# Hybrid RG-LRU, gMLP and gated FFN block: the up products of the FFN chained in single PSUM banks, split weights kept in DRAM

## The chip, the cores and the metric

One core of one Trainium2 chip runs the whole program once. The metric is device microseconds of an execution (us), the median over runs.

## The reference, cut to what matters

Tokens 2048, width 1024, inner FFN width 3072, float32 throughout. The mixer (RG-LRU and gMLP) makes x, and the FFN follows:

```python
y = concat(RMSNorm(y_lru), RMSNorm(y_gmlp)) @ W_out
x = x + gate_m * RMSNorm_post(y)
h = rmsnorm(x, g_ffn_pre) * (1.0 + sc_f) + sh_f      # sc_f, sh_f, gt_f: parts 3 to 5 of c_act @ w_ada
up = causal_depthwise_conv(h @ w_up, ffn_conv_w, ffn_conv_b)   # width 3
g_ff, v_ff = split(up, 2)                            # 3072 gate and 3072 value columns
y = (gelu(g_ff) * v_ff) @ w_down
x = x + gt_f * rmsnorm(y, g_ffn_post)
```

## The kernel before, in words

**Products.** A float32 operand is split into a high and a low part of a reduced type: a cast on ACT (`split`, L129) and a subtraction on DVE (L134). Each product of two operands is then three matmuls, high by high, high by low and low by high (`mm3`, L170 to L172; in the FFN L926 to L928), each 128x128 by 128x512.

**Stages.** The mixer works on four chunks of 512 tokens; its last product is `mixer_out` (tiles `o`), and the last two chunks leave their result in DRAM (`o2d`), to be normalized and added to x later by `late_rms` and `late_post` (tiles `ol`, L575, L576; result in `x2d`). The FFN works on two chunks C of 1024 tokens, each as two halves of 512 tokens. For each C come first 24 *pairs* (`up_pair`; f counts them), a gate block and a value block of 128 columns, whose result goes to DRAM (`gd`), then `down(C, 0)` and `down(C, 1)`, each 24 x 8 products that accumulate in eight banks.

**One pair.** Two halves of the tokens, two halves of the contraction and two column blocks are a 2x2 by 2x2 block product, made with seven products instead of eight (the scheme of Strassen and Winograd). On the side of the tokens it takes h11, h12, h22 and the sums s1 to s4, which `h2_task` makes once for each C: a load of x2d, the normalization (L840, L841), sums on DVE, splits. On the side of the weights it takes three blocks and four sums t1 to t4, which `up_weights` makes for each pair: two loads of 512 KB (`wug`, `wuv`; L900, L901), four sums on POOL (L905, L906, L910, L913), seven splits. A product is 4 x 3 matmuls, a pair 84. Results lie in two PSUM tiles `upa` and `upc` of two banks each, out of a pool of four such tiles (all eight banks). Three ACT copies and five DVE additions (L934 to L948) put them together to `Rg` and `Rv`; `conv` (L886 on ACT, L888 twice on DVE, L890 for the chunk's last two tokens), a gelu (L951), a product (L952) and the store to `gd` (L953) end the pair.

**Order.** The program is written with generators in the background (`start`), which `tick` advances by a step at fixed points of the main loop, and a scheduler orders each engine's instructions; `high_priority` moves loads and splits ahead. SP issues nearly all DMAs, in order. The main sequence stands at L1041 to L1072: h2_task(0, 0) beside the mixer's product for chunk 2, h2_task(0, 1) after that for chunk 3, then the pairs of C = 0 with `late_rms(3)` and `ada_task(5)` (the last part of c_act @ w_ada, eight steps on DVE, L268 and L270) in the background; the `late_post`s beside down(0, 0); the normalizers of chunks 2 and 3 and then h2_task(1, ...) beside down(0, 1).

Of the kernel before, what the change touches and what calls it, by code (L numbers as in the profile page):

```python
# [15 lines left out]
P = 128  # L16
# [7 lines left out]
NF = 24  # L24
# [16 lines left out]
def block_kernel(ctx: ExitStack, tc: tile.TileContext, xt, cols, rows, wada, wada_r, win_k, win_s, win_v, wgate, wsp, wout, wup, wdown, out):  # L41
# [8 lines left out]
    ps = ctx.enter_context(tc.tile_pool(name="ps", bufs=4, space=bass.MemoryType.PSUM))  # L50
# [209 lines left out]
    def ada_task(m, pause=0):  # L260
# [566 lines left out]

    H2 = {}
    OPS = ("11", "s2", "12", "s1", "s3", "s4", "22")

    def h2_task(C, i):

        ops = H2.setdefault(C, {o: [None, None] for o in OPS})
        r = [rx[2 * C], rx[2 * C + 1]]

        def get(t, j, name):
            x = load_x(x2d, 2 * C + t, j, name, t4)
            for b in range(2):
                d = 2 * j + b
                vec.scalar_tensor_tensor(out=x[:, b], in0=x[:, b], scalar=sf[:, d:d + 1], in1=r[t], op0=ALU.mult, op1=ALU.mult)  # L840
                act.activation(out=x[:, b], in_=x[:, b], func=AF.Identity, bias=shf[:, d:d + 1])  # L841
            return x

        def put(o, x):
            hl = h4(f"h{o}_{C}{i}h"), h4(f"h{o}_{C}{i}l")
            split(hl[0], hl[1], x, "act")
            ops[o][i] = hl

        n = f"xf{C}{i}"
        a11 = get(0, i, n + "a")  # L850
        put("11", a11)
        yield
        a21 = get(1, i, n + "b")
        yield
        a22 = get(1, i + 2, n + "c")
        put("22", a22)
# [286 lines left out]
```

## Time and profile before

| what | value |
|---|---|
| median of 3 runs | 2361.22 us (2359.91 to 2363.95) |
| the profiled execution | 2354.39 us |
| its span | 2352.6 us |
| its mean granted TensorE clock | 0.957 of full speed |
| PE busy | 2102.8 us, 89% of the span |
| DVE, ACT, POOL busy | 70%, 42%, 23% |

The profile shows one execution. The span runs from its first to its last instruction. Busy PE time is the union of matmuls whose records overlap, so the pace is read from start to start.

### The profile page before, as it was taken

Reading aid. Unit: us, or ns where it says so; the run is one execution under the profiler, and the core shown is the slowest. Engines: PE = TensorE matmul, PEld = TensorE weight load, DVE = VectorE, ACT = ScalarE, POOL = GpSimd, SP = SyncE. Lnnn points to the kernel's source line nnn. Section 1 sums busy time; section 2 is a strip of 40 time slices with the busy share of each in tenths; the row PEclk is TensorE's granted clock in tenths of the full one; section 3 lists DMA queues with packets and bytes.
Section 4 is the critical chain, followed back from the end, with each engine's and each line's share of the span. In section 5 each row is a group of like instructions: output and inputs, shape, how many; then the busy total and the mean of one; then the engine's idle time right before and its main releaser. Section 6 shows DMA issues by size and latency. Waiting matters only on the chain.

```text
span 2352.6 us, 23905 instructions
## 1 busy us (share of the span) xinstructions
PE 2102.8 (89%) x9008; PEld 1698.9 (72%) x9008; DVE 1643.5 (70%) x1854; ACT 986.8 (42%) x1226; POOL 541.2 (23%) x344
## 2 busy tenths in 40 slices
PE   4898979999777898999989989979999999899995
PEld 3786868788555677777777768857777777778784
DVE  7688797986637777787766668587777777643634
ACT  3464645425433434444443345434444444432422
POOL 4443434343112222222200100032322223000000
PEclk8999989999787999999999989989999999999997
DMA  7677587675441222222226736431222212344542
GB/s 297 240 289 262 187 298 278 228 260 197 173 159 63 72 90 77 76 81 72 90 99 224 259 107 245 149 116 66 78 72 81 75 69 81 102 140 152 196 154 72
DMA packets 117428, 354.32 MB, mean 151 GB/s; under 512 B 10816, under 2 KB 10944, under 8 KB 117312
## 3 DMA queue, kind: packets, MB, share of 16 engines
q1 hardware_dynamic: 110400, 327.62, 40.0%
q0 software_dynamic: 6912, 25.17, 2.8%
q8 instruction: 71, 1.16, 0.2%
q14 instruction: 45, 0.37, 0.1%
HBM read 281.45 MB, written 71.30 MB: 150 GB/s over the span
## 4 chain that ended last, share of the span: by engine, by line
PE 62%; DVE 24%; ACT 6%; issue 4%; DMA 4%; POOL 0%; SPq 0%; DVEq 0%; ACTq 0%; POOLq 0%
PE dn L170 7%; PE dn L171 7%; PE dn L172 7%; DVE a L888 6%; PE upc L926 6%; PE upc L928 6%; PE upc L927 5%; PE upa L926 4%; PE upa L927 4%; PE upa L928 4%; ACT a L886 2%; DVE w L134 1%; DVE Rv L946 1%; DVE Rg L948 1%; DVE ada_m L270 1%
## 5 line engine op out<-in xcount | busy, mean ns | idle before, releaser
L170 PE MATMUL dn<-gh,wd_h 128*128 128x512 f32 x768 | 301.3, 393 | 10.9 <-ACT wd_h L129 6.0
L171 PE MATMUL dn<-gl,wd_h 128*128 128x512 f32 x768 | 300.2, 392 | 0.0
L172 PE MATMUL dn<-gh,wd_l 128*128 128x512 f32 x768 | 277.3, 392 | 11.1 <-DVE wd_l L134 11.1
L134 DVE TENSOR_TENSOR wd_l<-wd_r,wd_h 128x1024 fp32r<-128x1024 f32 x96 | 121.0, 1260 | 195.3 <-ACT wd_h L129 186.0
L905 POOL TENSOR_TENSOR wt<-wuv,wug 128x512 f32<-128x512 f32 x48 | 64.6, 1347 | 836.6 <-DMA wuv<-in_wup_dram 583.3
L129 ACT CAST wd_h<-wd_r 128x1024 fp32r<-128x1024 f32 x96 | 101.3, 1056 | 252.4 <-PE dn L171 238.9
L129 ACT CAST wt<-wt 128x512 fp32r<-128x512 f32 x144 | 89.5, 621 | 268.1 <-PE upc L928 241.9
L172 PEld LDWEIGHTS dn<-gh,wd_l 128*128 128x128 f32 x768 | 145.4, 189 | 44.4 <-DVE wd_l L134 14.0
L170 PEld LDWEIGHTS dn<-gh,wd_h 128*128 128x128 f32 x768 | 145.3, 189 | 44.2 <-ACT wd_h L129 7.7
L888 DVE SCALAR_TENSOR_TENSOR a<-Rv,prm,a 128x1023 f32<-128x1023 f32 x96 | 154.4, 1608 | 19.4 <-ACT a L886 18.6
L171 PEld LDWEIGHTS dn<-gl,wd_h 128*128 128x128 f32 x768 | 145.3, 189 | 30.2
L888 DVE SCALAR_TENSOR_TENSOR a<-Rg,prm,a 128x1023 f32<-128x1023 f32 x96 | 123.1, 1282 | 36.5 <-ACT a L886 35.7
L134 DVE TENSOR_TENSOR w<-wug,w 128x512 fp32r<-128x512 f32 x96 | 76.8, 800 | 72.7 <-ACT w L129 72.7
L134 DVE TENSOR_TENSOR wt<-wt,wt 128x512 fp32r<-128x512 f32 x144 | 117.6, 817 | 9.5 <-ACT wt L129 8.7
L129 ACT CAST w<-wug 128x512 fp32r<-128x512 f32 x96 | 59.8, 622 | 123.8 <-PE upa L928 110.6
L913 POOL TENSOR_TENSOR wt<-wug,wt 128x512 f32<-128x512 f32 x48 | 69.4, 1445 | 92.7 <-DVE wt L134 92.7
L886 ACT ACTIVATE a<-Rg,prm 128x1024 f32<-128x1024 f32 x48 | 59.7, 1243 | 58.8 <-DVE Rg L948 57.6
L906 POOL TENSOR_TENSOR wt<-wuv,wt 128x512 f32<-128x512 f32 x48 | 77.7, 1618 | 3.5
L952 DVE TENSOR_TENSOR a<-a,a 128x1024 f32<-128x1024 f32 x48 | 59.6, 1241 | 24.8 <-ACT a L951 24.8
L926 PE MATMUL upc<-hs_10h,wt 128*128 128x512 f32 x96 | 39.6, 414 | 40.6 <-DVE Rg L948 35.6
L886 ACT ACTIVATE a<-Rv,prm 128x1024 f32<-128x1024 f32 x48 | 59.8, 1246 | 31.9 <-DVE Rv L946 28.3
L134 DVE TENSOR_TENSOR gl<-gr,gh 128x1024 fp32r<-128x1024 f32 x48 | 60.0, 1250 | 17.9 <-PE upc L928 9.3
(602 smaller groups left out, 5855.8 us busy)
## 6 DMA issues: line engine op xcount, KB each, us to landing
wd_r<-in_wdown_dram SPq DMA_DIRECT2D x96, 512.0 KB, 4.3
wug<-in_wup_dram SPq DMA_DIRECT2D x48, 512.0 KB, 3.2
wuv<-in_wup_dram SPq DMA_DIRECT2D x48, 512.0 KB, 3.3
gd<-a SPq DMA_DIRECT2D x48, 512.0 KB, 2.6
gr<-gd SPq DMA_DIRECT2D x48, 512.0 KB, 3.5
wada<-in_wada_r_dram SPq DMA_DIRECT2D x32, 512.0 KB, 4.3
win_h<-kept_s SPq DMA_DIRECT2D x30, 512.0 KB, 5.9
win_l<-kept_s SPq DMA_DIRECT2D x30, 512.0 KB, 6.7
```

The costliest lines, as they stand in the source:

```text
L129: act.copy(out=hi, in_=src)
L134: (leng or vec).tensor_tensor(out=lo, in0=src, in1=hi.bitcast(F32), op=ALU.subtract)
L170: pe.matmul(out=out, lhsT=wh, rhs=mh, start=first, stop=False)
L171: pe.matmul(out=out, lhsT=wh, rhs=ml, start=False, stop=False)
L172: pe.matmul(out=out, lhsT=wl, rhs=mh, start=False, stop=last)
L886: act.activation(out=a, in_=R, func=AF.Identity, scale=w[2], bias=col("ffn_conv_b", blk))
L888: vec.scalar_tensor_tensor(out=a[:, s:], in0=R[:, :FT - s], scalar=w[t], in1=a[:, s:], op0=ALU.mult, op1=ALU.add)
L906: pool.tensor_tensor(out=t2, in0=b22, in1=t1, op=ALU.subtract)
L913: pool.tensor_tensor(out=t2, in0=b21, in1=t2, op=ALU.subtract)
L926: pe.matmul(out=bank, lhsT=wh, rhs=mh, start=not more and k == 0, stop=False, skip_group_check=more)
L927: pe.matmul(out=bank, lhsT=wh, rhs=ml, start=False, stop=False, skip_group_check=more)
L928: pe.matmul(out=bank, lhsT=wl, rhs=mh, start=False, stop=k == 3, skip_group_check=more)
```

## The change

Five things, here in the order of the program:

1. **The end of the mixer.** `h2_task` becomes `h2_plain` (normalizes x, splits h11, h12, h21, h22, and stores the four normalized tiles to a new DRAM tensor `hs`, with DMAs that ACT issues) and `h2_sums` (loads them back and makes s1 to s4, for C = 0). h2_plain(0, 1) and h2_sums(0, 0) run beside mixer_out of chunk 3.
2. **Plain first pairs.** f = 0 and 1 of C = 0 are made by `up_plain` with eight products (96 matmuls), which need no sums; h2_sums(0, 1) runs beside them.
3. **Chained pairs.** For the FFN the PSUM pool is closed and a new one of eight single banks opened. A pair takes three banks. In the first, product 11 is copied out (m1), s2 t2 is added and the sum copied out (x0), s3 t3 is added and read by DVE (Rv), 22 t4 is added and copied out (Rg): each is the sum of what came before in the bank. The second takes s1 t1 (copy m5) and s4 22, the third 12 21. That is four ACT copies and three DVE additions a pair. `up_phase` interleaves one pair's end with the next pair's start.
4. **Kept pieces.** In C = 0, from f = 2, each of a pair's seven split pieces is stored to DRAM (`wkd`, 512 KB each). In C = 1, from f = 2, `up_weights` loads the seven pieces, with no sum and no split.
5. **Late work.** `late_rms(3)`, both `late_post`s, the normalizers of chunks 2 and 3 and ada_task(5) start at f = 3 of C = 0. h2_sums(1, 0) and h2_sums(1, 1) run beside down(0, 0) and down(0, 1). down uses eight single banks and evicts each by itself; ada transposes go in two halves.

The diff, cut to its core:

```diff
+    def h2_plain(C, i):
+        for q, (o, t, j) in enumerate((("11", 0, i), ("12", 0, i + 2), ("21", 1, i), ("22", 1, i + 2))):
+            x = normed(C, t, j, f"xf{C}{i}{o}")
+            put(C, i, o, x)
+            act.dma_start(out=hs[C, i, q], in_=x)
+            yield
+    def h2_sums(C, i, get, plain=()):
+        a21 = get(1, i, "21")
+        a22 = get(1, i + 2, "22")
...
+        vec.tensor_tensor(out=a22, in0=a22, in1=a21, op=ALU.add)
+        put(C, i, "s1", a22)
...
+    def from_store(C, i):
+        def get(t, j, o):
+            x = lp.tile([P, 2, 512], F32, tag="ld", name=f"hs{C}{i}{o}")
+            sync.dma_start(out=x, in_=hs[C, i, ("11", "12", "21", "22").index(o)])
...
     def up_weights(C, f):
+        if C == 1 and f >= PLAIN:
+                for q, k in enumerate(PIECES):
...
+                    sync.dma_start(out=w[k].bitcast(F32), in_=wkd[f, q])
+            return w
...
+        if C == 0:
+            for q, k in enumerate(PIECES):
+                sync.dma_start(out=wkd[f, q], in_=w[k].bitcast(F32))
...
+    def up_pair(C, f):
+        w = up_weights(C, f)
+        pa = bank(f"upa{n}")
+        prod(C, pa, "11", w["11"])
+        act.copy(out=m1, in_=pa)
+        pc = bank(f"upc{n}")
+        prod(C, pc, "s1", w["t1"])
+        act.copy(out=m5, in_=pc)
+        yield
+        prod(C, pa, "s2", w["t2"], more=True)
+        act.copy(out=x0, in_=pa)
+        pb = bank(f"upb{n}")
+        prod(C, pb, "12", w["21"])
+        vec.tensor_tensor(out=Rg[:, :512], in0=pb, in1=m1, op=ALU.add)
+        prod(C, pc, "s4", w["22"], more=True)
+        vec.tensor_tensor(out=Rv[:, :512], in0=pc, in1=x0, op=ALU.add)
+        prod(C, pa, "s3", w["t3"], more=True)
+        vec.tensor_tensor(out=Rv[:, 512:], in0=pa, in1=m5, op=ALU.add)
+        v = conv(C, NF + f, Rv)
+        yield
+        prod(C, pa, "22", w["t4"], more=True)
+        act.copy(out=Rg[:, 512:], in_=pa)
...
-    drain(*lt)
-    drain(*start(h2_task(0, 1)))
-    start(late_rms(NC - 1, q), ada_task(5, 2))
+    nt = start(h2_plain(0, 1), h2_sums(0, 0, from_store(0, 0)))
+    O, q3 = mixer_out(NC - 1, True)
+    drain(*lt, *nt)
+    mixer_ps.close()
+    banks.append(ctx.enter_context(tc.tile_pool(name="pf", bufs=8, space=bass.MemoryType.PSUM)))
+    st = start(h2_sums(0, 1, from_store(0, 1)))
+    for f in range(PLAIN):
...
+        up_plain(0, f)
+    drain(*st)
+    up_phase(0, PLAIN, lambda f: start(late_chunks(), ada_task(5, 1)) if f == PLAIN + 1 else None)
```

**PE, between two pairs of C = 0.** The names give tile, chunk and pair: `upc0_15` is the second PSUM tile of pair 15, `hs1_00h` the high part of s1. Before, from pair 15 to pair 17, which share a PSUM tile (the first two products of pair 16 stand ahead of these rows):

```order
L926 MATMUL upc0_15_6947<-hs3_00h_4347,wt3_0_15_6936 128x512 [waits Activation_49]
...
L926 MATMUL upc0_15_6947<-hs4_00h_4431,w22_0_15_6939 128x512 [waits DVE_49]
...
L926 MATMUL upc0_15_6947<-h22_00h_4235,wt4_0_15_6943 128x512 [waits DVE_49]
...
L928 MATMUL upc0_15_6947<-h22_01h_4737,wt4_0_15_6943 128x512
L926 MATMUL upc0_17_7227<-hs1_00h_4270,wt1_0_17_7212 128x512 [waits DVE_49,Activation_49]
```

And now, around the start of pair 16:

```order
L971 MATMUL upa0_16_7340<-h11_00h_4153,w11_0_16_7308 128x512 [waits PE_49]
L972 MATMUL upa0_16_7340<-h11_00l_4154,w11_0_16_7308 128x512
L971 MATMUL upa0_15_7191<-hs3_00h_4674,wt3_0_15_7177 128x512 [waits Activation_49]
...
L973 MATMUL upa0_16_7340<-h11_00h_4153,w11_0_16_7308 128x512 [waits DVE_49]
...
L971 MATMUL upc0_16_7355<-hs1_00h_4543,wt1_0_16_7312 128x512
...
L971 MATMUL upa0_15_7191<-h22_00h_4290,wt4_0_15_7181 128x512 [waits DVE_49]
...
L971 MATMUL upa0_16_7340<-hs2_00h_4634,wt2_0_16_7316 128x512 [waits Activation_49]
...
L971 MATMUL upc0_16_7355<-hs4_00h_4744,w22_0_16_7323 128x512 [waits Activation_49]
...
L971 MATMUL upa0_16_7340<-hs3_00h_4674,wt3_0_16_7326 128x512 [waits Activation_49]
```

Before, the first product of pair 17 stood directly behind the last of pair 15 in the same tile. Now two to three other products stand between any product of a bank and the next one in that bank, which waits for the bank's reader.

**ACT, from the mixer's last product to the first pair.** `oo3_2` and `oo3_3` are the copies of that product out of PSUM, `rp3` its squares, `w11_0_1` and the like weight pieces. Before:

```order
L551 COPY oo3_2_4645<-o3_2_4588 128x1024
L208 ACTIVATE rp3_s2_4647<-oo3_2_4645 128x1024 [waits Activation_49]
...
L551 COPY oo3_3_4708<-o3_3_4651 128x1024 [waits DVE_49]
L208 ACTIVATE rp3_s3_4710<-oo3_3_4708 128x1024 [waits Activation_49]
L841 ACTIVATE xf01a_1_4714<-xf01a_1_4714,modc_103 128x512 [waits DMAHW0_49,DVE_49]
```

And now:

```order
L136 CAST hs3_00h_4674<-hs0011_4592 128x1024
L559 COPY oo3_2_4708<-o3_2_4644 128x1024
...
L136 CAST hs4_00h_4744<-hs0012_4706 128x1024 [waits DVE_49]
L559 COPY oo3_3_4776<-o3_3_4714 128x1024
L215 ACTIVATE rp3_s3_4778<-oo3_3_4776 128x1024 [waits Activation_49]
L136 CAST hs1_01h_4791<-hs0122_4788 128x1024 [waits DVE_49]
L992 COPY R20_0_4811<-up200_0_4812 128x512 [waits PE_49]
```

Before, the copy `oo3_3` stood ahead of all work on the second half of h. Now it stands behind the split of s4 (`hs4_00h`), and the first plain product (`up200_0`) is copied soon after it.

**SP, the DMAs of one pair of C = 0.** Before (three a pair):

```order
L900 DMA wug0_18_7336<-in_wup_dram 128x1024 [waits DMAHW0_49,DMAHW6_49,DVE_49,Pool_49]
L953 DMA gd_99<-a0_14_6897 128x1024 [waits DVE_49]
L901 DMA wuv0_18_7337<-in_wup_dram 128x1024 [waits DMAHW2_49,DVE_49]
L900 DMA wug0_19_7476<-in_wup_dram 128x1024 [waits DMAHW1_49,DMAHW3_49,DVE_49,Pool_49]
L953 DMA gd_99<-a0_15_7048 128x1024 [waits DVE_49]
```

And now (ten a pair):

```order
L963 DMA wkd_4098<-w11_0_16_7308 128x1024 [waits DMAHW0_49,DVE_49]
L963 DMA wkd_4098<-wt1_0_16_7312 128x1024 [waits DMAHW1_49,DVE_49]
L963 DMA wkd_4098<-wt2_0_16_7316 128x1024 [waits DMAHW2_49,DVE_49]
L963 DMA wkd_4098<-w21_0_16_7319 128x1024 [waits DMAHW3_49,DVE_49]
L928 DMA wug0_18_7601<-in_wup_dram 128x1024 [waits DMAHW4_49,Pool_49]
L963 DMA wkd_4098<-w22_0_16_7323 128x1024 [waits DMAHW5_49,DVE_49]
L978 DMA gd_99<-a0_14_7234 128x1024 [waits DMAHW6_49,DVE_49]
L963 DMA wkd_4098<-wt3_0_16_7326 128x1024 [waits DMAHW7_49,DVE_49]
L929 DMA wuv0_18_7602<-in_wup_dram 128x1024 [waits DMAHW0_49]
L963 DMA wkd_4098<-wt4_0_16_7330 128x1024 [waits DMAHW1_49,DVE_49]
```

Each pair's seven stores stand among the loads for the pair two later, and every DMA waits for the one eight before it on its semaphore.

## Rows read from the trace of the kernel before

**Rows 1.** The page: span, busy time, the chain that ended last.

```profile
span 2352.6 us, 23905 instructions
PE 2102.8 (89%) x9008; PEld 1698.9 (72%) x9008; DVE 1643.5 (70%) x1854; ACT 986.8 (42%) x1226; POOL 541.2 (23%) x344
...
PE 62%; DVE 24%; ACT 6%; issue 4%; DMA 4%; POOL 0%; SPq 0%; DVEq 0%; ACTq 0%; POOLq 0%
```

**Rows 2.** The timeline of PE in down(0, 1) (start, length, instruction).

```profile
1500.20 0.39 PE L170 MATMUL dn<-gh,wd_h 128*128 128x512 f32 x1
1513.12 0.39 PE L170 MATMUL dn<-gh,wd_h 128*128 128x512 f32 x1
```

**Rows 3.** The timeline of PE, one matmul nineteen pairs apart.

```profile
1618.07 0.47 PE L926 MATMUL upc<-hs_10h,wt 128*128 128x512 f32 x1 [1.68 <-DVE Rg L948]
2021.76 0.47 PE L926 MATMUL upc<-hs_10h,wt 128*128 128x512 f32 x1 [1.27 <-DVE Rg L948]
```

**Rows 4.** Waits of PE over the span (total, times, longest).

```profile
PE upc L926 <- DVE Rg L948: 71.2, 42, 4.2
```

**Rows 5.** Windows (us; PE, PEld, DVE, ACT, POOL busy; clock; DMA share; GB/s).

```profile
571.25:616.00 44.75, 44.71 (x199) 36.69 (x197) 37.63 (x35) 17.90 (x20) 10.24 (x4) 1.00 0.63 222
616.00:682.20 66.20, 48.64 (x194) 38.73 (x195) 22.61 (x22) 22.26 (x26) 10.79 (x5) 0.82 0.43 151
682.20:724.00 41.80, 14.58 (x37) 9.69 (x36) 21.99 (x24) 17.87 (x23) 3.60 (x2) 0.59 0.26 88
724.00:773.70 49.70, 42.36 (x172) 33.41 (x170) 40.64 (x42) 17.54 (x26) 17.00 (x11) 0.93 0.20 69
953.90:1201.90 248.00, 234.02 (x1016) 188.13 (x1016) 196.27 (x231) 111.82 (x156) 61.90 (x45) 1.00 0.23 81
1237.00:1526.00 289.00, 271.99 (x1165) 220.93 (x1165) 184.48 (x172) 122.33 (x129) 19.59 (x10) 0.98 0.59 200
1526.00:1595.30 69.30, 52.83 (x207) 40.52 (x206) 57.33 (x61) 24.84 (x38) 26.38 (x15) 0.90 0.29 99
100.00:120.00 20.00, 20.00 (x90) 16.57 (x89) 15.21 (x14) 10.38 (x11) 14.61 (x12) 1.00 0.96 344
```

**Rows 6.** Timeline of PE at the end of the mixer and in the first pair.

```profile
628.40 0.80 PE L170 MATMUL o<-rl3h,wout_h 128*128 128x512 f32 x1 [12.44 <-ACT rl3h L129]
694.00 0.80 PE L926 MATMUL upa<-h_01h,w 128*128 128x512 f32 x1 [8.91 <-ACT h_01h L129]
718.89 0.80 PE L926 MATMUL upa<-hs_00h,wt 128*128 128x512 f32 x1 [10.15 <-ACT px L934]
```

**Rows 7.** DMA issues (line, engine, count, KB each, us to landing).

```profile
wug<-in_wup_dram SPq DMA_DIRECT2D x48, 512.0 KB, 3.2
gd<-a SPq DMA_DIRECT2D x48, 512.0 KB, 2.6
x2d<-oo SPq DMA_DIRECT2D x8, 512.0 KB, 6.0
xf01d<-x2d SPq DMA_DIRECT2D x1, 512.0 KB, 7.7
```

**Rows 8.** Groups of DVE, 953.9 to 1201.9 (busy, mean ns, idle before).

```profile
L134 DVE TENSOR_TENSOR wt<-wt,wt 128x512 fp32r<-128x512 f32 x36 | 28.9, 803 | 4.2 <-ACT wt L129 4.0
L888 DVE SCALAR_TENSOR_TENSOR a<-Rv,prm,a 128x1023 f32<-128x1023 f32 x12 | 24.7, 2058 | 3.7 <-ACT a L886 3.6
L946 DVE TENSOR_TENSOR Rv<-upc,px 128x512 f32<-128x512 f32 x12 | 8.3, 688 | 2.2 <-PE upc L928 1.9
```

**Rows 9.** Groups of DVE, 773.7 to 932 and 1237 to 1526.

```profile
L270 DVE SCALAR_TENSOR_TENSOR ada_m<-wada,cact,ada_m 128x1024 f32<-128x1024 f32 x4 | 9.6, 2395 | 0.0
...
L575 DVE SCALAR_TENSOR_TENSOR ol<-ol,gm,rp_r 128x512 f32<-128x512 f32 x16 | 11.3, 748 | 14.6 <-DMA ol<-o2d 14.6
L576 DVE TENSOR_TENSOR ol<-ol,xr 128x1024 f32<-128x1024 f32 x8 | 9.8, 1222 | 0.1
L196 DVE RECIPROCAL rq_r<-rq_r 128x512 f32<-128x512 f32 x2 | 6.5, 3296 | 0.0
```

**Rows 10.** Timeline of PE in down(0, 0) and in the first pairs of C = 1.

```profile
1406.39 0.80 PE L172 MATMUL dn<-gh,wd_l 128*128 128x512 f32 x1 [6.90 <-DVE wd_l L134]
1553.28 0.79 PE L926 MATMUL upc<-h_10h,wt 128*128 128x512 f32 x1 [5.17 <-DVE Rv L946]
```

More of the change, by code (lines that the diff above doesn't have):

```diff
@@ L65, in psum, with bank @@
         return ps.tile([P, 2, 512], F32, tag="ps", name=name)
+    banks = []
+    def bank(name):
+        return banks[0].tile([P, 512], F32, tag="pf", name=name) if banks else psum(name)[:, 0]
     def bc2(ap):
@@ L828, in block_kernel @@
     H2 = {}
[L829 to L856, printed above, removed]
+    PLAIN = 2
@@ new lines, in block_kernel, with put, normed @@
+    hs = dram.tile([NFC, 2, 4, P, 2, 512], F32, name="hs")
+    wkd = dram.tile([NF, 7, P, 2, 4, P], F32, name="wkd")
+    def put(C, i, o, x):
+        hl = h4(f"h{o}_{C}{i}h"), h4(f"h{o}_{C}{i}l")
+        split(hl[0], hl[1], x, "act")
+        H2.setdefault(C, {}).setdefault(o, [None, None])[i] = hl
+    def normed(C, t, j, name):
+        x = load_x(x2d, 2 * C + t, j, name)
+        for b in range(2):
+            d = 2 * j + b
+            vec.scalar_tensor_tensor(out=x[:, b], in0=x[:, b], scalar=sf[:, d:d + 1], in1=rx[2 * C + t], op0=ALU.mult, op1=ALU.mult)
+            act.activation(out=x[:, b], in_=x[:, b], func=AF.Identity, bias=shf[:, d:d + 1])
+        return x
@@ new lines, in up_weights, with prod @@
+        if C == 0:
+            for q, k in enumerate(PIECES):
+                sync.dma_start(out=wkd[f, q], in_=w[k].bitcast(F32))
+        return w
+    def prod(C, pt, a, w, first=True, last=True, more=False):
+        for k in range(4):
+            hi, lo = H2[C][a][k // 2]
+            wh, wl, mh, ml = w[:, 0, k], w[:, 1, k], hi[:, k % 2], lo[:, k % 2]
+            pe.matmul(out=pt, lhsT=wh, rhs=mh, start=first and not more and k == 0, stop=False, skip_group_check=more)
+            pe.matmul(out=pt, lhsT=wh, rhs=ml, start=False, stop=False, skip_group_check=more)
+            pe.matmul(out=pt, lhsT=wl, rhs=mh, start=False, stop=last and k == 3, skip_group_check=more)
@@ L1006, in down @@
         for f in range(2):
-            for d in range(6, 8):
-                mm(f, d)
+            mm(f, 7)
         for f in range(2, NF - 2):
@@ L1039, in down, with late_chunks @@
         done.append(final())
+    def late_chunks():
+        yield from late_rms(NC - 1, q3)
+        for c in (NC - 2, NC - 1):
+            yield
+            yield from late_post(c)
+            yield
+            rx[c] = rms_bcast(rq[c], 1.0, f"rq{c}")
     nt = start(mixer_norm(NC - 1, 2))
@@ L1043, in block_kernel @@
         tick()
-    nt += start(h2_task(0, 0))
+    nt += start(h2_plain(0, 0))
     O, q = mixer_out(NC - 2, True)
```

198 lines of the change are left out of this document (106 added, 92 removed).

## The prediction, blind

> **What bounds the kernel now.** The page comes first [rows 1]: PE is busy for 2102.8 of 2352.6 us and has the largest share of the chain that ended last, 62%. So a gain has to come from time in which PE waits or runs at a low clock. That PE's records overlap shows in the next view: at [rows 2] 57 matmuls start in 1513.12 - 1500.20 = 12.92 us, so at full clock a 128x512 matmul costs **0.227 us**, not the 0.39 of its record, and the 84 of a pair cost 19.04 us. Against that floor each stage is read.
>
> In the steady part of the second up stage [rows 3], 19 pairs take 2021.76 - 1618.07 = 403.7 us, 21.25 each, 2.2 above the floor. In the first up stage the twelve pairs of 953.9 to 1201.9 [rows 5] take 20.67, 1.6 above it. The waits say why [rows 4]: 42 times, for 71.2 us in all (1.7 each), the first product of a pair waits for the DVE addition that reads the last product of the pair two before out of the same PSUM tile. DVE is busy for 196.27 of those 248 us [rows 5], so it comes late but does not bound.
>
> The windows of the stages [rows 5] show the rest. Around the end of the mixer, 571.25 to 773.7, only 209 up matmuls (37 + 172) are done after 682.2, worth 47.4 us at full clock, in 91.5 us; the clock is 0.82, then 0.59, the lower of the two levels (1.2 and 2.4 GHz) for most of the time. The gaps are in [rows 6]: 12.44 us before chunk 3's mixer product, then, inside the first pair, 8.91 us for the normalized tile h_01 and 10.15 us behind the sums. At the start of the second up stage, 207 matmuls (46.9 us) take 69.3 us [rows 5], where down's final work holds DVE [rows 10].
>
> **The change part by part.** The sum is made against the profiled execution's 2354.4 us; the median, 2361.2, lies 6.8 above, and that is added at the end.
>
> *End of the mixer to the first pairs.* Work on the second half of h now runs beside mixer_out of chunk 3, so nothing waits for sums in the first two pairs. The 12.44 us gap [rows 6] should close, since ACT's cast for it stands behind less; The 194 matmuls of 616 to 682 [rows 5] are 44 us at full clock; with 2 for waits I let the mixer product end at 662 instead of 682. What is late next stands on ACT: the copy oo3_3 is behind the split of s4, and that behind a chain of DRAM round trips (x2d loads, hs stores, hs loads) through three load buffers. A store of such a tile lands after up to 6.0 us and a load after up to 7.7 [rows 7], and the first plain product needs the banks that oo3_3 frees. Two round trips past the end, less what overlaps, make an estimate of 18 us idle (ends: 6, a single load; 30, two stores and two loads and a bit). Plain pairs start at 680 and take 192 x 0.227 = 43.5 us, and 2.5 at a low clock, to 726. At 773.7 the old kernel has 24 x 84 - 209 = 1807 matmuls left; the new one has 24 more in all (2040), so it is there after 233, at 726 + 41 x 0.227 = 735. **Minus 38** (-28 to -48).
>
> *The rest of the first up stage.* The 1807 matmuls are 410 us at full clock, and took 463 (773.7 to 1237). The DVE wait of [rows 4] goes: the order shows 23 to 36 matmuls (5.2 to 8.2 us) of other products between a bank's product and the next that needs its reader, and that reader takes 0.69 us [rows 8]. The waits that come in its place I cost at nothing in the steady part; the cover is those products, and a reader queued more than 5 us deep would end it (first rival). DVE's load: 196.27 / 12 = 16.35 us a pair, less two additions of 0.69 is 14.98, under 19.04. But from f = 3 to 10 the late work joins: 8 x 14.98 = 119.8, eight ada steps of 2.4 (19.2), both late_posts (11.3 + 9.8), three reciprocals (9.8), and about 5 for small splits [rows 9], in all 175 us against 152 of PE: 23 over. Of DMA, ten 512 KB transfers a pair are 5.24 MB in 19.04 us, 275 GB/s, where this kernel has moved 344 GB/s over 20 us at a share of 0.96 [rows 5]. With the late work, the pairs 2 to 11 issue 131 transfers (68.7 MB), 199 us at that rate for 190 us of PE: 9 over. The two excesses added are 32 us of loss (ends: 10, if buffers even them out; 60, if they come on top of a slower rate). With 3 us of transitions: 410 + 35 against 463, **minus 18** (+10 to -40).
>
> The Trainium skill, page "DMA: Bandwidth & Descriptors", section "Anatomy of one DMA — SWDGE (gpsimd) path", gives a DMA a fixed cost of about 2 us, mostly the write receipt and heaviest toward HBM, which speaks against this many DRAM stores; by its fit one store here would take an estimated 3.2 us, where the row has 2.6.
>
> *Down of the first chunk.* 1165 matmuls (264 us) took 289 [rows 5]; the posts leave DVE, and with them the 6.90 us wait behind them [rows 10], while h2_sums takes their place. **Minus 8** (-14 to +5).
>
> *The second up stage.* Before: 69.3 us for the first 207 matmuls, then 21.5 pairs of 21.25, together 527 us against 457 at full clock, a loss of 70. After: DVE has no split and POOL no sum from f = 2, so DVE falls to about 16.35 - 7 x 0.80 - 2 x 0.69 = 9.4 us a pair [rows 8], and eight transfers (4.19 MB) a pair ask 220 GB/s; each load is issued nine or more products (24 us) ahead of its use, and lands in 3 to 8 [rows 7]. I leave 10 us of loss at the transition (the finals still stand on DVE) and 3 elsewhere: **minus 57** (-64 to -45).
>
> A smaller gain on the side: the first L888 on Rv takes 2058 ns in [rows 8] beside POOL's sums, and would lose some of it where they are gone; DVE is not the bound there, so it is counted at nothing. The halved ada transposes and single evictions I also cost at nothing: they lie under 0.23 us x 576 matmuls of a down half.
>
> **The sum.** -38 - 18 - 8 - 57 = -121; 2354.4 - 121 = 2233 for a profiled execution, **2240 us** for the median.
>
> **Rivals.** *Chained waits stall as the old one did.* Each chain has four waits a pair, and ACT and DVE serve their queues in order behind splits of 0.6 to 0.8 us and convolutions of 1.2 to 2.1 [rows 8]. If one of them costs the old 1.7 us in each of 44 pairs, less the eight that DVE bounds anyway, 36 x 1.7 = 61 comes back: **2301**. For it: DVE at 79% busy already came late. Against: 5 us of cover, where the old order had none. Chance 0.2.
>
> *Buffers even out the late zone, and the mixer's gap is short.* Loss 10 instead of 32, idle 8 instead of 18: **2208**. For it: the late work is spread by ticks, and DVE's excess is 15%. Chance 0.18.
>
> *Transfers come nearly one after the other.* If SP's in-order queue, which now waits for each split before its store, leaves little overlap, a pair costs 8 x 2.6 + 2 x 3.2 = 27.2 us [rows 7] instead of 19.04. Over 22 pairs that is +180, with 21 late transfers of some 4 us +84, less the 32 counted: 2240 + 232 = **2472**, slower. It turns the sign once a pair takes over 19.04 + 121 / 22 = 24.5 us, which is 214 GB/s. For it: a store lands in 2.6 us, 202 GB/s alone. Against: 344 GB/s in [rows 5], in a stretch of loads and kept stores, so transfers do overlap. Chance 0.05.
>
> The Trainium skill, page "DMA: Bandwidth & Descriptors", section "Where 436 GB/s comes from", puts the limit of a core toward HBM at about 358 GB/s; the row's 344 agrees, and by it the late zone would be 192 us of DMA instead of 199.
>
> *The change doesn't do what it says*, the gap at the mixer's end growing and the late zone stretching until little is left, somewhere near 2355: chance 0.02.
>
> **How the numbers follow.** The forecast has 0.55. The range takes in the second rival with the good ends of down and the last stage (2208 - 6 - 7 = 2195) and the first with a few us of a slower DMA rate (2305): the forecast's first up stage runs from 680 to 1180, and its 247 transfers (129 MB) would take 565 us instead of those 500 at 229 GB/s, which gives 2305 too. About two in ten lie outside. A change under 0.2%, 4.7 us, could not be told from none. Faster 0.93 (forecast, both first rivals, most of what lies between), same 0.02, slower 0.05.
>
> **What would show it.** A pair of the steady first stage in 19.0 to 19.3 us, and the second stage the same from f = 2; no row of PE waiting for the Rg addition; one gap of 10 to 25 us between the last o and the first plain product, ended by ACT; pairs 3 to 10 at some 23 us with DVE over 95% busy; a DMA rate of 260 to 290 GB/s in the first up stage. Pairs above 24 us with SP's queue as the releaser, or many waits of over 1 us for m1, m5, x0 or Rv, would make the prediction wrong.

## The result and the profile after

The changed kernel takes **2221.76 us** (median of 4 runs, 2220.21 to 2222.51) against 2362.49 of the old one in runs on the same chip: a ratio of 0.9405, 95% interval 0.9388 to 0.9421. The forecast was 2240 in a range of 2195 to 2305. The profiled execution took 2222.20 us. Its page: span, busy time, and the chain that ended last (before: [rows 1]).

```profile
span 2220.4 us, 24098 instructions
PE 2072.0 (93%) x9032; PEld 1700.7 (77%) x9032; DVE 1435.9 (65%) x1598; ACT 928.8 (42%) x1154; POOL 424.8 (19%) x248
...
PE 73%; DVE 14%; ACT 4%; DMA 4%; issue 4%; POOL 1%; SPq 0%; DVEq 0%; ACTq 0%; POOLq 0%
```

24 more matmuls take 30.8 us less of busy PE, while the mean granted clock rose from 0.957 to 0.971; DVE's share of the chain fell from 24% to 14%.

The experiments ran on other chips, where the old kernel took 2365 to 2370 us. So a difference of a few us between medians of two experiments is held against the ratios (each to the old kernel on the same chip) and the stages before it is believed.

The stages, in us of the profiled executions, are read from PE's timeline: first product `o` of chunk 2, first up product, ends of the up and down stages. Where two stages interleave at a border, each matmul there counts as 0.227. All kernels run here stand in one table; e1 to e12 are the experiments below.

| kernel | to o of chunk 2 | to first up | up C = 0 | down C = 0 | up C = 1 | rest | span |
|---|---|---|---|---|---|---|---|
| before | 571.3 | 111.0 | 556.0 | 287.6 | 531.8 | 295.0 | 2352.6 |
| after | 577.0 | 104.8 | 509.6 | 264.2 | 471.7 | 293.0 | 2220.4 |
| e1 no kept pieces | 574.6 | 104.4 | 500.2 | 263.5 | 474.8 | 293.4 | 2211.0 |
| e2 no plain pairs | 579.0 | 107.5 | 520.9 | 264.4 | 472.2 | 292.9 | 2236.9 |
| e3 late work back | 576.5 | 104.9 | 468.8 | 279.8 | 472.4 | 293.0 | 2195.3 |
| e4 ada whole | 574.4 | 108.9 | 508.3 | 264.4 | 472.4 | 293.0 | 2221.4 |
| e5 late work spread | 577.2 | 104.7 | 483.5 | 264.6 | 472.3 | 293.2 | 2195.5 |
| e6 chain alone | 572.8 | 110.7 | 523.1 | 286.4 | 498.6 | 293.5 | 2285.1 |
| e7 = e1 + e5 | 577.4 | 104.4 | 470.5 | 263.5 | 474.3 | 293.5 | 2183.7 |
| e8 = e7, sums later | 572.3 | 99.8 | 485.7 | 264.0 | 474.5 | 293.2 | 2189.5 |
| e9 stored twice | 577.4 | 105.8 | 601.7 | 273.6 | 471.9 | 293.1 | 2323.4 |
| e10 = e7, own sums | 576.8 | 106.0 | 472.1 | 263.5 | 471.7 | 293.8 | 2183.8 |
| e11 = e10 + e8 + 3 plain | 573.1 | 99.5 | 473.2 | 263.7 | 472.0 | 293.0 | 2174.7 |
| e12 = e6, other bank | 574.1 | 110.6 | 498.6 | 283.3 | 477.1 | 294.9 | 2238.6 |

Of the change's 132.2 us of span, 46.4 lie in the first up stage, 23.4 in the first down stage and 60.1 in the second up stage. The medians differ by more, 140.7, because the old kernel's profiled execution lay 8.1 us under its median.

The timeline of DVE shows one product of gate and value twenty pairs apart in C = 1: (1901.01 - 1520.21) / 20 = 19.04 us, the floor of 84 matmuls, where it was 21.25 [rows 3].

```profile
1520.21 1.22 DVE L977 TENSOR_TENSOR a<-a,a 128x1024 f32<-128x1024 f32 x1
1901.01 1.22 DVE L977 TENSOR_TENSOR a<-a,a 128x1024 f32<-128x1024 f32 x1
```

The windows of the stages (columns as in [rows 5]): in the steady parts, third and fifth row, PE is never idle and at full clock.

```profile
726.00:1005.00 279.00, 250.95 (x1045) 202.21 (x1045) 240.55 (x256) 134.62 (x189) 100.17 (x55) 0.95 0.79 292
805.00:960.00 155.00, 127.22 (x498) 100.45 (x498) 137.02 (x138) 71.87 (x101) 66.41 (x35) 0.91 0.75 282
1005.00:1186.00 181.00, 181.00 (x800) 149.90 (x799) 138.28 (x164) 95.81 (x137) 47.64 (x33) 1.00 0.74 275
1191.50:1455.70 264.20, 262.54 (x1156) 216.37 (x1155) 142.09 (x132) 109.71 (x126) 5.12 (x4) 1.00 0.50 171
1520.00:1927.00 407.00, 407.00 (x1798) 336.99 (x1797) 188.60 (x259) 129.02 (x152) 0.00 (x0) 1.00 0.64 218
```

Waits of PE over the span: the wait on Rg of [rows 4] is gone. The new readers of the chained banks (the ACT copies to m1, m5 and x0, the DVE addition to Rv) are waited for once each, 9.8 us in all.

```profile
PE o L177 <- DVE modc L285: 18.1, 1, 18.1
PE upc L971 <- ACT wt L136: 14.8, 4, 8.8
...
PE up L971 <- ACT oo L559: 7.8, 1, 7.8
...
PE upc L971 <- ACT m L1008: 5.5, 1, 5.5
...
PE upa L971 <- ACT m L1004: 2.5, 1, 2.5
...
PE upa L971 <- ACT x L1012: 1.2, 1, 1.2
...
PE upa L971 <- DVE Rv L1020: 0.6, 1, 0.6
```

What is left on PE's timeline: the start of the plain pairs, the worst gap of the late zone, and the first pairs of C = 1.

```profile
681.87 0.80 PE L971 MATMUL up<-h_00h,w 128*128 128x512 f32 x1 [7.85 <-ACT oo L559]
924.52 0.80 PE L971 MATMUL upc<-hs_00h,w 128*128 128x512 f32 x1 [5.50 <-ACT m L1008]
1488.00 0.80 PE L971 MATMUL upc<-hs_10h,wt 128*128 128x512 f32 x1 [8.78 <-ACT wt L136]
```

The first up stage still loses 509.6 - 2040 x 0.227 = 47 us, nearly all of it between 726 and 1005, where the late work runs. There the clock is at 0.95 and DVE busy for 240.55 of 279 us, 86%. PE waits twelve times there, all between 804 and 939, for 28.0 us in all, and a clock of 0.95 over 279 us is worth another 14. The largest of these waits, in the window 726 to 1005:

```profile
PE upc L971 <- ACT wt L136: 6.0, 3, 3.3
PE rq_m L199 <- DVE rq_hl L140: 5.6, 2, 3.0
PE upc L971 <- ACT m L1008: 5.5, 1, 5.5
PE upc L973 <- DVE wt L141: 4.9, 2, 3.7
```

They are weight pieces that come late, the two late normalizers (`rq`), and the three ACT copies. The timeline of ACT shows the copy to m5 itself waiting behind DVE's work on `ol`, which is late_post:

```profile
923.88 0.58 ACT L1008 COPY m<-upc 128x512 f32<-128x512 f32 x1 [1.60 <-DVE ol L583]
```

### The profile page after: what moved, and what is told of

Read it like the earlier page. It is cut to its first block, busy times and chain, and to the rows that moved or that the text cites. A ratio compares the mean times of both kernels' runs of the same rounds, so it can differ in the third digit from the quotient of the medians.

```text
span 2220.4 us, 24098 instructions
## 1 busy us (share of the span) xinstructions
PE 2072.0 (93%) x9032; PEld 1700.7 (77%) x9032; DVE 1435.9 (65%) x1598; ACT 928.8 (42%) x1154; POOL 424.8 (19%) x248
## 4 chain that ended last, share of the span: by engine, by line
PE 73%; DVE 14%; ACT 4%; DMA 4%; issue 4%; POOL 1%; SPq 0%; DVEq 0%; ACTq 0%; POOLq 0%
PE dn L177 8%; PE dn L178 8%; PE dn L179 8%; PE upa L973 7%; PE upa L972 7%; PE upa L971 7%; PE upc L973 3%; PE upc L972 3%; PE upc L971 3%; PE upb L973 2%; PE upb L971 2%; PE upb L972 2%; PE lg L177 1%; PE lg L178 1%; PE lg L179 1%
## 5 line engine op out<-in xcount | busy, mean ns | idle before, releaser
L179 PE MATMUL dn<-gh,wd_l 128*128 128x512 f32 x768 | 265.0, 389 | 0.0
L918 DVE SCALAR_TENSOR_TENSOR a<-Rv,prm,a 128x1023 f32<-128x1023 f32 x92 | 121.9, 1325 | 38.7 <-ACT a L916 38.5
L951 POOL TENSOR_TENSOR wt<-wuv,wug 128x512 f32<-128x512 f32 x24 | 39.3, 1637 | 523.7 <-DMA wuv<-in_wup_dram 411.7
L136 ACT CAST wt<-wt 128x512 fp32r<-128x512 f32 x72 | 44.7, 622 | 113.3 <-PE upa L973 39.5
L141 DVE TENSOR_TENSOR wt<-wt,wt 128x512 fp32r<-128x512 f32 x72 | 62.7, 873 | 24.0 <-ACT wt L136 23.8
L976 ACT ACTIVATE a<-a 128x1024 f32<-128x1024 f32 x48 | 50.9, 1061 | 53.7 <-DVE a L923 31.9
L1020 DVE TENSOR_TENSOR Rv<-upa,m 128x512 f32<-128x512 f32 x46 | 31.6, 687 | 58.3 <-PE upa L973 58.3
L136 ACT CAST gh<-gr 128x1024 fp32r<-128x1024 f32 x48 | 50.8, 1058 | 13.3 <-DMA gr<-gd 6.1
L1024 ACT COPY Rg<-upa 128x512 f32<-128x512 f32 x46 | 26.8, 584 | 69.7 <-PE upa L973 69.7
L959 POOL TENSOR_TENSOR wt<-wug,wt 128x512 f32<-128x512 f32 x24 | 39.9, 1662 | 82.4 <-DVE wt L141 55.5
```

The lines of the kernel that those rows point to most:

```text
L136: act.copy(out=hi, in_=src)
L141: (leng or vec).tensor_tensor(out=lo, in0=src, in1=hi.bitcast(F32), op=ALU.subtract)
L179: pe.matmul(out=out, lhsT=wl, rhs=mh, start=False, stop=last)
L918: vec.scalar_tensor_tensor(out=a[:, s:], in0=R[:, :FT - s], scalar=w[t], in1=a[:, s:], op0=ALU.mult, op1=ALU.add)
L976: act.activation(out=g, in_=g, func=AF.Gelu_apprx_tanh)
```

## The experiments

**e1 and e9: what the kept pieces bring, and what a store costs.** e1 takes the kept pieces away:

```diff
-        if C == 1 and f >= PLAIN:
+        if False:
...
-        if C == 0:
-            for q, k in enumerate(PIECES):
-                sync.dma_start(out=wkd[f, q], in_=w[k].bitcast(F32))
```

> The changed kernel without the kept pieces: no wkd store in C = 0, and C = 1 loads and splits its weights as C = 0 does. Theory: the second up stage's gain (531.8 to 471.7 us) comes from the chained banks, since the steady pairs of C = 0, which still split, already run at 19.0 to 19.3 us; so C = 1 stays near 19.1 a pair and loses at most 10 us at its start, and the late zone of C = 0, with 154 stores fewer, gains 5 to 15. Total 2210 to 2230 against 2222. Rival: the kept pieces carry that gain, because DVE comes late again with the splits back; then the pairs of C = 1 go to 20.6 or more, 22 x 1.6 = 35 us, total about 2257.

Measured: 2213.72 us, ratio 0.9351 (0.9331 to 0.9372), faster than the change itself. The second up stage is 3.1 us longer, the first 9.4 shorter. In the steady part of C = 1 (window of e1) PE is never idle although DVE now splits, busy for 325.33 of 380 us:

```profile
1520.00:1900.00 380.00, 380.00 (x1678) 314.67 (x1677) 325.33 (x380) 194.48 (x280) 137.93 (x77) 1.00 0.25 86
```

So the kept pieces take load off DVE where none has to be taken off, and their stores cost 9 us in the first up stage. They cost little without the late work beside them: e3 below keeps the stores, moves most of that work away, and has a first up stage of 468.8 us, 6 above the 463 of its matmuls. e9 adds stores, to price them:

```diff
                 sync.dma_start(out=wkd[f, q], in_=w[k].bitcast(F32))
+                sync.dma_start(out=wk2[f, q], in_=w[k].bitcast(F32))
```

> The changed kernel that stores each kept piece twice, to two DRAM tensors (154 stores more, nothing else): the price of DMA traffic by itself. A steady pair of C = 0 then asks 17 transfers, 8.9 MB, which in 19.05 us would be 468 GB/s. Theory: transfers overlap up to the 344 GB/s that a 20 us window of the old kernel showed, or a little more, so a pair takes 22 to 26 us, and over 22 pairs 65 to 150 us come on top: total 2285 to 2370. Rival (the slower side of the prediction): transfers come nearly one after the other, 15 stores of 2.6 us and two loads of 3.2, 45 us a pair: above 2700. If the total stays near 2222, stores cost nothing here, and the 9 us that the kept pieces cost in the first up stage are not DMA.

Measured: 2325.28 us (one run), with steady pairs of 23.9 us. Two windows of e9, one in the late zone and one over eleven steady pairs:

```profile
755.00:813.00 58.00, 52.53 (x228) 42.15 (x226) 34.35 (x42) 24.34 (x34) 6.78 (x5) 0.99 1.03 410
1010.00:1270.00 260.00, 223.86 (x920) 168.88 (x919) 154.74 (x195) 103.94 (x153) 60.34 (x41) 0.99 0.97 372
```

In the steady pairs DMA is busy nearly all the time, at a share of 0.97 and 372 GB/s; 17 transfers in 23.9 us are 373 GB/s. The 410 of the first window show that 372 is no ceiling; why the steady pairs stay below it was not tested. Transfers overlap, and the slower rival, which has them one after the other at some 200 GB/s, is refuted. The change's own rates, 275 GB/s (0.74) in the steady part and 292 (0.79) from 726 to 1005, lie well below both. So how the kept pieces' stores delay PE in the late zone is not shown; a DMA rate at its limit, on average, it is not.

**e6 and e12: the chain by itself.** e6 is the old kernel, with late work and down as they were and no plain pairs, but with chained and interleaved pairs in the old pool of two-bank tiles and the weight pieces made in another order:

```diff
+        T, U = psum(f"upa{n}"), psum(f"upc{n}")
+        pa, pb, pc = T[:, 0], T[:, 1], U[:, 0]
```

> The old kernel with nothing changed but the pairs: chained and interleaved as in the change, in the old pool of four two-bank tiles (11 and 12 21 in the two banks of one, s1 in the other), with t1 made ahead of t2. Theory: the chaining removes the wait on Rg, so steady pairs go to 19.0 to 19.3 us in both up stages; the second falls from 531.8 by 40 to 50, the first from 556 by 25 to 40, the rest stays: total 2275 to 2300 against 2362. Rival: the eight single banks are what lets the pairs overlap, and with two-bank tiles the wait only moves to another product: total above 2330.

Measured: 2287.53 us, ratio 0.9659 (0.9639 to 0.9679). The total is the theory's, the pairs are not: 20.1 us, between the two. The timeline of e6 shows why:

```profile
1645.11 0.39 PE L930 MATMUL upa<-h_11h,w 128*128 128x512 f32 x1
...
1645.53 0.69 DVE L946 TENSOR_TENSOR Rg<-upa,px 128x512 f32<-128x512 f32 x1 [1.32 <-PE upa L930]
...
1646.28 0.50 PE L928 MATMUL upa<-hs_10h,wt 128*128 128x512 f32 x1 [0.78 <-DVE Rg L946]
```

The waits of e6 say that it happens 42 times:

```profile
PE upa L928 <- DVE Rg L946: 34.4, 42, 2.3
```

Product 12 21 ends in bank 1 of tile `upa`, DVE reads it, and s3 t3, which goes to bank 0 of the same tile, starts only after that read; whether the chip would need that wait, or only the program holds it, the traces don't tell. e12 puts 12 21 beside s1:

```diff
-        pa, pb, pc = T[:, 0], T[:, 1], U[:, 0]
+        pa, pb, pc = T[:, 0], U[:, 1], U[:, 0]
```

> e6_chain_alone with one letter changed: product 12 21 goes to the second bank of the other tile, beside s1, instead of beside 11. Theory: e6's pairs stand at 20.1 us because s3 t3 waits 0.78 us, once a pair, until DVE has read 12 21, which lies in the other bank of the same tile and was finished just ahead; the waiting is by tile, not by bank. With 12 21 elsewhere that wait goes, pairs run at 19.0 to 19.3, and 44 pairs x 0.9 = 40 us come back: 2240 to 2255. Rival: the chain itself needs the third tile, and another of its waits takes the place of this one: 20 us a pair still, 2275 or more.

Measured: 2240.33 us, ratio 0.9465 (0.9440 to 0.9489), pairs of 19.0 to 19.1 on average in both steady parts, and that wait is gone from the list of e12's waits; what is left of its kind there is

```profile
PE upa L928 <- DVE Rv L948: 3.0, 4, 0.9
```

The edit did more than its one letter says, since the scheduler then ordered the products anew. In e6 s3 t3 stands directly behind 12 21. The timeline of e12 has s1 t1 of the next pair between them, and s4 22, which now shares the tile of 12 21, two products (5.4 us) behind it:

```profile
1649.14 0.39 PE L928 MATMUL upc<-h_10h,w 128*128 128x512 f32 x1
...
1651.86 0.39 PE L928 MATMUL upc<-hs_10h,wt 128*128 128x512 f32 x1
...
1654.58 0.39 PE L928 MATMUL upa<-hs_10h,wt 128*128 128x512 f32 x1
...
1657.30 0.39 PE L928 MATMUL upc<-hs_10h,w 128*128 128x512 f32 x1
```

So e6 shows that a product waited for the reader of the other bank of its tile, and e12 that the wait goes when the two products in one tile stand apart; a different order in e6's tiles might have done the same.

Chained and interleaved pairs in this order, without single banks, bring 5.35 per cent by themselves, where the whole change brings 5.95. What the chain does and what the interleaving does was not separated: both put other products between a reader and the next write into its bank.

**e3 and e5: the late work.** e3 puts both late_posts, their normalizers and chunk 1's sums back to the first down stage (the core of the edit):

```diff
-    up_phase(0, PLAIN, lambda f: start(late_chunks(), ada_task(5, 1)) if f == PLAIN + 1 else None)
+    up_phase(0, PLAIN, lambda f: start(late_rms(NC - 1, q3), ada_task(5, 1)) if f == PLAIN + 1 else None)
...
+    posts = start(late_post(2), late_post(3))
+    down(0, 0)
```

> The changed kernel with both late_posts, their normalizers and all of chunk 1's sums back in the first down stage, as before the change; late_rms(3) and ada_task(5) stay in the first up stage. Theory: the first down stage's unforeseen gain (287.6 to 264.2 us) comes from that work leaving DVE, so it goes back by 15 to 25 us, while the first up stage (509.6) loses its late zone's worst part and falls by 20 to 30: total 2207 to 2227. Rival: the single-bank tiles and evictions of down carry that gain; then down stays within 5 us of 264 and the total falls to 2195 to 2205.

Measured: 2197.39 us, ratio 0.9280 (0.9262 to 0.9298). The total is the rival's, the stages are the theory's: down goes back up by 15.6 us, and a wait of the old kind [rows 10] is there again in its timeline, but the first up stage falls by 40.8, more than either said.

```profile
1311.12 0.80 PE L179 MATMUL dn<-gh,wd_l 128*128 128x512 f32 x1 [7.33 <-DVE wd_l L141]
```

e5 leaves the late work in the up stage, thinner:

```diff
+    def slow(g, n):
+        for _ in g:
+            yield from wait(n)
...
-start(late_chunks(), ada_task(5, 1))
+start(slow(late_chunks(), 2), ada_task(5, 2))
```

> The changed kernel with the late work spread thinner: the steps of late_chunks at every second tick, ada_task(5) with a pause of 2 instead of 1, so that it lies over some 16 pairs instead of 8. Theory: the 47 us that the first up stage loses against full clock lie in the late zone, where DVE has more to do than a pair's 19.04 us hold; spread out it fits into the 4 us a pair that DVE has free, and 20 to 35 us come back: total 2187 to 2202. Rival: the loss is the latency of the late chain itself (PE waits in order for its two normalizers, weights split late behind it), which a thinner spread moves but does not shorten: total 2215 to 2222.

Measured: 2197.40 us, ratio 0.9282 (0.9265 to 0.9300), with 26.1 us less in the first up stage and nothing given back in down. The window of e5, to be held against the first of the change's windows above:

```profile
726.00:1005.00 279.00, 270.09 (x1171) 221.21 (x1170) 250.21 (x263) 142.85 (x206) 113.83 (x59) 0.99 0.85 311
```

DVE does more in the same 279 us (250.21), DMA moves more (311 GB/s), and PE still has 126 more matmul records. So over the late zone as a whole neither was at its limit in the change: the steps stood too close together, and PE, in order, stopped twelve times and ran at 0.95 of its clock, where e5 has 0.99. The rival, a latency that spreading only moves, would have left the total at 2215 or more, and falls.

**e7: both.** e1 and e5 together.

> The changed kernel without the kept pieces and with the late work spread thinner, both at once. Theory: the kept pieces' stores and the late work burden the late zone separately (DMA and DVE), so the two gains, 8 and 24 us, add: 2186 to 2194. Rival: both relieve the same queue, and the sum is no better than the spread alone: 2195 to 2200; or DVE, which now splits in C = 1 too, costs there what it saves: above 2200.

Measured: 2184.98 us, ratio 0.9223 (0.9207 to 0.9239). They add, as far as the intervals tell (the ratio falls by 0.0182, and e1 and e5 by themselves give 0.0177): the first up stage takes 470.5 us, some 7 above the 463 of its matmuls at full clock.

**e2: no plain pairs.**

```diff
-    for f in range(PLAIN):
...
-        up_plain(0, f)
...
-    up_phase(0, PLAIN, lambda f: start(late_chunks(), ada_task(5, 1)) if f == PLAIN + 1 else None)
+    up_phase(0, 0, lambda f: start(late_chunks(), ada_task(5, 1)) if f == PLAIN + 1 else None)
```

> The changed kernel without the two plain pairs: f = 0 and 1 of C = 0 are seven-product pairs too (24 matmuls, 5.4 us, fewer), so the first of them needs the sums s1 to s4 of both halves of h. Theory: the plain pairs hide the sums of the second half; without them a gap of the old kind comes back (8.91, 7.23 and 10.15 us stood there before, with a low clock behind them), 20 to 40 us less the 5.4: total 2237 to 2257. Rival: the sums would be ready nearly in time anyway, now that the first half's run beside the mixer's product, and the plain pairs only cost their 5.4 us: about 2216 to 2222.

Measured: 2233.10 us, ratio 0.9426 (0.9402 to 0.9450). The medians are 11 us apart, the ratios 0.0021 (5 us), with intervals that overlap; so the plain pairs earn 5 to 11 us net of their own 5.4, less than the theory's 15 to 35, and the sign is likely but not certain. Waits of e2 from 670 to 780 show what came back:

```profile
PE upa L971 <- ACT oo L559: 11.7, 1, 11.7
PE upc L971 <- ACT wt L136: 8.5, 1, 8.5
```

The copy oo3_3 is waited for 4 us longer than in the change, and then a weight piece on ACT for 8.5; no wait for the sums themselves is on the list.

**e4: the ada transposes whole.**

```diff
+        if not banks:
+            pt = psum(f"adaps_m{m}").rearrange("p a (b c) -> p (a b) c", c=P)
...
-        for q in range(2):
+        for q in range(2 if banks else 0):
```

> The changed kernel with the ada transposes of the mixer part in one PSUM tile again, as before (the halves stay in the FFN part). Theory: the halves take two of the four two-bank tiles, and the 18.13 us wait of the mixer product on the ada reduction at 290.8 us is the cost; the mixer's end, 5.8 us later than before the change (577.04 against 571.25), comes back by 4 to 6 us: total 2216 to 2218. Rival: those 5.8 us come from elsewhere in the mixer, and the total stays at 2222.

Measured: 2223.21 us, ratio 0.9395 (0.9376 to 0.9415): no difference. The timeline of e4 tells where the gain went:

```profile
312.71 0.77 PE L199 MATMUL rl_m<-rl_hl,onesD 128*128 128x512 f32 x1 [10.65 <-DVE rl_hl L140]
683.28 0.80 PE L976 MATMUL up<-h_00h,w 128*128 128x512 f32 x1 [12.07 <-ACT oo L564]
```

The 18.13 us wait is replaced by one of 10.65, and the mixer's end is 2.6 us earlier; then the first plain product waits 12.07 us instead of 7.85 and starts at 683.28. So that start hangs on ACT's chain, not on the mixer's products alone.

**e8, e10, e11: the two gaps that are left.** e8 moves the first half's sums off that chain:

```diff
-    nt = start(h2_plain(0, 1), h2_sums(0, 0, from_store(0, 0)))
+    nt = start(h2_plain(0, 1))
...
+    def both():
+        for i in range(2):
+            yield from h2_sums(0, i, from_store(0, i))
```

> e7_no_keep_spread with the sums of the first half of h moved from beside the mixer's last product to beside the two plain pairs, one after the other with the second half's. Theory: the first plain product waits 7 to 8 us for the copy oo3_3, which ACT does behind the split of s4, and that behind a chain of DRAM round trips; with the sums out of the way the copy follows the mixer's product at once, and 5 to 7 us go: 6 under e7. Rival: the two halves' sums no longer fit into the plain pairs' 44 us, and the first seven-product pair waits for s1 or s2 instead: 5 us or more over e7.

Measured: 2194.14 us, ratio 0.9263 (0.9245 to 0.9282): the rival's total. Its timeline has both halves of the story: 1.91 us instead of 7.5 ahead of the plain pairs, and 10.76 at the first chained pair's s1 t1, ended not by a sum, as the rival had it, but by ACT's cast of a weight piece.

```profile
672.16 0.50 PE L967 MATMUL up<-h_00h,w 128*128 128x512 f32 x1 [1.91 <-ACT oo L559]
...
729.49 0.79 PE L967 MATMUL upc<-hs_00h,wt 128*128 128x512 f32 x1 [10.76 <-ACT wt L136]
```

e10 goes at the start of the second up stage. In e7's timeline the chain of that wait is plain: POOL waited 31.93 us until down's final had freed a load tile, then summed, ACT cast, PE went on.

```profile
1445.30 4.39 POOL L950 TENSOR_TENSOR wt<-wuv,wug 128x512 f32<-128x512 f32 x2 [31.93 <-DVE fo L1109]
1447.50 0.62 ACT L136 CAST wt<-wt 128x512 fp32r<-128x512 f32 x1 [6.16 <-POOL wt L950]
1448.17 0.80 PE L967 MATMUL upc<-hs_10h,wt 128*128 128x512 f32 x1 [8.78 <-ACT wt L136]
```

```diff
-            t = lp.tile([P, 2, 4, P], F32, tag="ld", name=f"wt{n}")
+            own = C == 1 and f < 3
+            t = tp.tile([P, 2, 4, P], F32, tag="t4", name=f"wt{n}") if own else lp.tile([P, 2, 4, P], F32, tag="ld", name=f"wt{n}")
```

> e7_no_keep_spread with the weight sums of the first three pairs of C = 1 in tiles of another pool than the loads of down's final. Theory: the 8.78 and 4.38 us waits at the start of the second up stage come from POOL's first sum, which waits 31.9 us until the final has freed the three load tiles; with tiles of their own the sums are early and 9 to 13 us go: 2172 to 2177 against 2185. Rival: DVE and ACT are behind by the final's work there anyway, and the wait only changes its name: 2182 to 2186.

Measured: 2183.12 us, ratio 0.9227 (0.9212 to 0.9241), not to be told from e7. The sum is early now, as e10's timeline shows, but PE waits for other pieces, behind the final's work on DVE:

```profile
1421.55 1.27 POOL L951 TENSOR_TENSOR wt<-wuv,wug 128x512 f32<-128x512 f32 x1 [295.06 <-DVE fs L1074]
...
1428.36 0.79 PE L970 MATMUL upc<-hs_10h,wt 128*128 128x512 f32 x1 [3.93 <-DVE wt L141]
```

e11 adds e8's edit and a third plain pair (`PLAIN = 3`, with which the late work starts a pair later too):

> e10_own_sums with the sums of both halves of h beside the plain pairs (as in e8) and three plain pairs instead of two (12 matmuls, 2.7 us, more). Theory: the first plain product starts 5 to 6 us earlier, as in e8, and the sums, which came 10.75 us late there, are now ready by the first seven-product pair: 2 to 4 us under e10. Rival: the sums still come late, and it is 3 us or more over e10.

Measured: **2176.65 us**, ratio 0.9200 (0.9185 to 0.9215), the fastest kernel here, 45 us under the change; 6.5 under e10, more than expected. The first up product starts at 672.66, where e10 has 682.79, and PE waits for no sum. Part of that is not the edit's: the first `o` of chunk 2, ahead of what it touches, is 3.7 us earlier too. Its page:

```profile
span 2174.7 us, 23881 instructions
...
PE 2059.8 (95%) x9044; PEld 1694.0 (78%) x9044; DVE 1598.1 (73%) x1746; ACT 1007.0 (46%) x1305; POOL 587.2 (27%) x332
```

## Why the prediction was right, and where it was not

The forecast lies 18 us above the result, well inside its range. Against the profiled executions the sum said -121 where -132 was measured; the other 7 us are the 6.8 added for the median, since the new kernel's profiled execution (2222.20) lies at its median. The main mechanism, the wait on Rg gone and PE at its floor in the steady pairs, was right. That the sum came so close is in part luck, since misses of both signs are in it: the first down stage gained 15 us more than forecast, the second up stage 3 and the end 2, while the first up stage (with the end of the mixer) gained 4 less and 6 were lost ahead of it.

*The bound.* PE was the bound, and its waits were worth what was put down. The wait on Rg went, and in the steady parts the cover of 5 to 8 us held, and pairs reached 19.04 us. So the first rival fell for the steady parts. In the late zone it came true in small: there the copies to m1, m5 and x0 were late, for 9.2 us. e6 shows too that it was no idle fear, since one product with no cover costs 1 us a pair. e12 shows the chained and interleaved pairs to be the main cause.

*End of the mixer to the rest of the first up stage.* -38 and -18 were forecast, 56 together; the table has -6.1 and -46.4, 52.5. Inside it two errors cancel. The mixer's last product ended at 674, not 662: 5.8 of these 12 us lie ahead of its first product, and the rest in two waits of 1.82 and 2.15 us and a clock of 0.94 from 616 to 674. The idle time after it was 7.85 us, not 18, below the 10 to 25 that were to be the sign. So the plain pairs began at 681.9 where 680 was forecast. e4 and e8 confirm the reason given for that start. The late zone lost more than the 32 us put down: 47, less the 5.5 counted for clock and transitions, is some 42. Its DMA part, 9, has the size of what e1 gave back (9.4), but not by the working given: it was to come from transfers at a limit of 344 GB/s, and the zone moved 292 at a share of 0.79. Its DVE part, 23, was undersized, and the mechanism behind it off: DVE was to be over 95% busy with pairs of some 23 us, and from 805 to 960 it was at 88% with pairs of 26 (498 matmuls in 155 us); and e5 fits the same work in and loses 26 us less. Not throughput failed there, but the distance between the steps. The second rival was right on the idle time (8) and wrong on the late zone (10).

*Down of the first chunk.* Forecast -8, measured -23.4: the largest miss. The step that failed took the 6.90 us wait of [rows 10] and a little beside it for all that the posts cost there. e3 puts them back with the sums and down rises by 15.6 us, of which that wait is under half. The remaining 8 us, which e3's down keeps, are not split further.

*The second up stage.* Forecast -57, measured -60.1, a hit by its size but not by its working, which put DVE's relief first: e1 shows the stage at 474.8 us without the kept pieces, so they bring 3.1 of the 60.1.

*Counted at nothing.* Up to the first `o` of chunk 2 the new kernel is 5.8 us later. The timelines split this at the mixer's first product `u`; the rows are from the kernel before, the change and e4, in this order:

```profile
129.24 0.50 PE L170 MATMUL u<-x0hi,win_h 128*128 128x512 f32 x1 [0.52 <-ACT r L371]
131.86 0.50 PE L177 MATMUL u<-x0hi,win_h 128*128 128x512 f32 x1 [0.52 <-ACT r L379]
132.09 0.50 PE L177 MATMUL u<-x0hi,win_h 128*128 128x512 f32 x1 [0.52 <-ACT r L384]
```

From there to the first `o` of chunk 2 the three take 442.0, 445.2 and 442.3 us. The four kernels with whole transposes lie between 442.0 and 442.5, the ten with halved ones between 443.9 and 445.9. So the halved transposes, which take two of the four tiles, cost 2 to 3 us. The other 2.6 of the 5.8 lie ahead of `u`, where kernels with the same mixer code differ by as much as 6 (127.4 in e8, 133.6 in e7). The single evictions cost nothing that shows.

*The slower rival.* Stores do overlap (e9). To turn the sign, it would have needed a rate of 214 GB/s or less; e9 moved 372 to 410.

## What to carry to other kernels

Where an in-order engine is the bound, look at what stands between a result and the next write into the same tile: 3 to 8 us of other products hid nearly every reader here, none cost 1 to 2 us each time, and two banks that share a tile can wait for each other. Relieving an engine that keeps up (DVE at 86% in e1) bought next to nothing, and the traffic that it took had its own price; undo such a part by itself before keeping it. Side work that fits by its sum can still stop the main engine where its steps stand close together. Spreading it over all the room that there is, and moving most of it to another stage, gave the same total here (2197.40 in e5, 2197.39 in e3).

## What the runs showed of the hardware

DMA between this core and DRAM ran at 372 GB/s over 260 us, at a share of 0.97, with most of the transfers 512 KB stores (e9), and in the same run at 410 GB/s over 58 us. The old kernel's busiest stretch quoted here had 344 at 0.96 [rows 5], which the forecast took for the limit. The Trainium skill, page "DMA: Bandwidth & Descriptors", section "Where 436 GB/s comes from", puts the DRAM side's limit at about 358 GB/s a core, half of what two cores share. Here one core runs, the measured 372 and 410 are above it, and the measurement decides.

A store of 512 KB to DRAM landed after 2.6 us in the old kernel [rows 7]; in the new one the page's DMA issues give

```profile
wkd<-wt SPq DMA_DIRECT2D x88, 512.0 KB, 4.0
wkd<-w SPq DMA_DIRECT2D x66, 512.0 KB, 3.7
...
gd<-a SPq DMA_DIRECT2D x48, 512.0 KB, 3.9
```

and with 275 GB/s moving none of it shows in PE's time in the steady part (181.00 us busy of 181.00).
